# Moving the weight blocks' casts and low parts behind the instruction that follows the former block's last product

## The chip, the cores and the metric

The kernel runs on one core of one Trainium2 chip. The metric is the device time of one execution in microseconds. TensorE (PE) multiplies, VectorE (DVE) and ScalarE (ACT) do elementwise work, SyncE (SP) issues the loads, and all run side by side, each through its own list of instructions.

## What is computed

A block of two layers on 256 latent and 256 context tokens, model width 1024. In each layer: a SwiGLU FFN at half step, four token mixers side by side (attention, Fourier, a convolution module, a short gated convolution) that are merged by gates, and a second FFN at half step. Each part is normalised and modulated first. In short:

```python
def ffn_half(x, mod, slot, g, w13, w2):
    h = modulated_norm(x, mod, slot, g)
    a, b = jnp.split(h @ w13, 2, axis=-1)
    return x + 0.5 * mod[:, :, 3 * slot + 2] * ((jax.nn.silu(a) * b) @ w2)
...
    gates = jax.nn.sigmoid(g + lw['b_gate']).reshape(B, L, N_BRANCHES, D_MODEL)
    merged = gates[:, :, 0] * y_a + gates[:, :, 1] * y_b + gates[:, :, 2] * y_c + gates[:, :, 3] * y_d
    return merged @ lw['w_o']
```

The context tokens are a prefix of the same trunk; the last layer's mixer and FFN produce the latent tokens alone. All weights are float32.

## The kernel before

Activations lie with channels on the partitions and tokens along the free axis, 512 columns (latent and context) in layer 0 and in the first FFN of layer 1, 256 behind it (258 in the last FFN, which carries two columns more for a late normalisation).

**Weight blocks.** A product in float32 precision is made from three faster ones. A block of weights is 128 x 1024, 512 KB. `wblock` (L177) loads it into `raw` (L179, on SyncE's queue), ScalarE casts it to the rounded type as `whi` (L181), and VectorE subtracts that from `raw` and so makes the low part `wlo` (L183). `mm3` (L187 to L189) then multiplies `whi` with the activation's high part, `whi` with its low part, and `wlo` with its high part. There are four buffers for `raw` and six each for `whi` and `wlo`: the cast of a block can be written once the last product has been done that reads the block six before it. There are 408 blocks.

**FFN.** `ffn` (L565) goes through the 22 tiles of the hidden width in three parts. In each part `project` (L493) takes pairs of blocks, one for the a half and one for the b half of a tile: TensorE multiplies both, then ScalarE takes the Silu of a (L583) and VectorE multiplies it with b (L593), and the product is split into high and low part (L193 on ScalarE, L194 on VectorE). Then `down` (L517) multiplies the part with eight w2 blocks and VectorE adds to the residual stream (L372). `down` has no instruction on ScalarE other than casts, and squares in the last part. In the last FFN the evacuation begins with a multiplication by the late normalisation's factor and a copy of a statistic, both on VectorE (L468, L470), and only then has the Silu its input.

**Mixer.** The mixer of a layer multiplies the input projections, then merges four branches (`merge`, L999): for each output tile a gate projection, whose Tanh is taken on ScalarE (L1011), a product of the branch with a `w_br` block, and the gating on VectorE (L1032, L1036). Attention is pumped in between as a job in steps: a query's scaling and rotary embedding, its split into two halves with DMAs (L868 to L870), scores on TensorE (L896), the row maximum and its negation on VectorE (L900, L903), Exp on ScalarE (L908), reciprocal and scaling on VectorE (L911, L912), transposes on TensorE (L923), copies on ScalarE (L927), values on TensorE (L940).

**Filler.** The modulations of later parts are computed along the way (`ada_later`): VectorE multiplies and sums weight tiles (L318), TensorE adds up rows with a matmul on ones (L297), ScalarE copies the sums (L327), and TensorE transposes them (L331).

**What sets the order.** The code is recorded in program order, and a scheduler then decides from dependencies and its own estimate of times in which order each engine gets its instructions; in the first stretch, up to the first FFN's first pairs, the order on TensorE and SyncE is written by hand. On the chip each engine keeps the order it was given. In the order before, a block's cast stands about where its load is expected to have landed, before or behind other work of ScalarE, as the scheduler finds it best.

Of the kernel before, what the change touches and what calls it, by code (L numbers as in the profile page):

```python
# [14 lines left out]
ALU = mybir.AluOpType  # L15
# [5 lines left out]
KD = D // P  # L21
# [59 lines left out]
def hybrid_block(ctx: ExitStack, tc: tile.TileContext, a, out, dbg=None):  # L81
    nc = tc.nc
# [8 lines left out]
    def nm(s):  # L91
        uid[0] += 1
        return f"{s}_{uid[0]}"
# [79 lines left out]
    def load_tables():  # L173
        nc.sync.dma_start(out=rope_c, in_=a["rope_c"])
        nc.sync.dma_start(out=rope_s, in_=a["rope_s"])

    def wblock(src, n=1024):  # L177
        raw = wp.tile([P, 1024], F32, tag="raw", name=nm("raw"), bufs=RINGS["raw"])
        nc.sync.dma_start(out=raw[:, :n], in_=src)  # L179
        hi = wp.tile([P, 1024], F32R, tag="whi", name=nm("whi"), bufs=RINGS["whi"])  # L180
        nc.scalar.copy(hi[:, :n], raw[:, :n])  # L181
        lo = wp.tile([P, 1024], F32R, tag="wlo", name=nm("wlo"), bufs=RINGS["wlo"])
        nc.vector.tensor_tensor(out=lo[:, :n], in0=raw[:, :n], in1=hi[:, :n], op=ALU.subtract)  # L183
        return hi, lo

    def mm3(ps, wh, wl, xh, xl, first, last):
        nc.tensor.matmul(ps, lhsT=wh, rhs=xh, start=first, stop=False)  # L187
# [170 lines left out]
    def cols(s):  # L358
        return slice(s * S, (s + 1) * S)
# [133 lines left out]
    def project(units, u, T, evac, group=1, halves=False, mid=None):  # L493

        for g in range(0, len(units), group):
            some = [(name, src if isinstance(src, list) else [src]) for name, src in units[g : g + group]]
            for i in range(max(len(src) for _, src in some)):
                ws = [wblock(src[i]) for _, src in some]  # L500
                if i == 0:
                    pss = [pmm() for _ in some]
                for n, c in enumerate([cols(s) for s in range(2)] if halves else [slice(0, T)]):
                    o = slice(c.start + i * T, c.stop + i * T)
                    turns = [(k, w) for k in range(KD) for w in zip(ws, pss)]
                    if n == 1:
                        turns = [(k, w) for w in zip(ws, pss) for k in range(KD)]
                    for k, ((hi, lo), ps) in turns:
                        if mid and k == KD // 2:
                            mid()  # L510
                            mid = None
                        kc = slice(k * P, (k + 1) * P)
                        mm3(ps[:, o], hi[:, kc], lo[:, kc], u[k][0][:, c], u[k][1][:, c], k == 0, k == KD - 1)
            for (name, _), ps in zip(some, pss):
                evac(name, ps)

    def down(blocks, parts, NB, G, last, nxt, group=1, filler=None):  # L517
# [12 lines left out]
        for g, count in starts:  # L530
            ws = [blocks(m) for m in range(g, g + count)]
            pss = [pmm() for _ in ws]
            if count == 1:
                mms(ws[0], pss[0], whole)
            else:
                for k in range(n):
                    kc = slice(k * P, (k + 1) * P)
                    for w, ps in zip(ws, pss):
                        mm3(
                            ps[:, whole], w[0][:, kc], w[1][:, kc], parts[k][0][:, whole], parts[k][1][:, whole],  # L540
                            k == 0, k == n - 1,
                        )
            for i, ps in enumerate(pss):
                for s in range(NB):
                    residual(g + i, s, ps, G, last)
                if last and NB == 1:
                    nxt.tile(g + i)
            if not last and filler:
                filler(count)
        if not last:  # L550
            return
        if split_last:
            ws = [blocks(m) for m in range(m1, KD)]
            pss = [pmm() for _ in ws]
            for s in range(2):
                for i, (w, ps) in enumerate(zip(ws, pss)):
                    mms(w, ps, cols(s))
                    residual(m1 + i, s, ps, G, True)
                nxt.stat(s)
            nxt.apply(0)  # L560
        else:
            nxt.stat(0)
            nxt.apply(0)
# [59 lines left out]
    def mixer(l, NB, norm, nxt, filler):  # L623
# [375 lines left out]
        def merge(b, parts, rate, t=0):  # L999
# [4 lines left out]
            for m0 in range(0, KD, per_unit):  # L1004
# [16 lines left out]
                for i, m in enumerate(ms):  # L1021
                    if m % per == 0:
                        blocks = wblock(a["w_br"][l, 2 * b + (m // per) if b < 3 else 6 + m // per])
                    hi, lo = blocks
                    o = ps[:, i * T : (i + 1) * T]
                    for k in range(nk):
                        c = ((m % per) * nk + k) * P
                        xh, xl = parts[k]
                        mm3(o, hi[:, c : c + P], lo[:, c : c + P], xh[:, :T], xl[:, :T], k == 0, k == nk - 1)

                tot = total[m0 // per_unit]
                nc.vector.scalar_tensor_tensor(  # L1032
# [30 lines left out]
    first = []  # L1063
# [4 lines left out]
    def begin_first(ns, ks):  # L1068
        for k in ks:
            kc = slice(k * P, (k + 1) * P)  # L1070
            for n in ns:
                (hi, lo), ps = first[n]
                mm3(ps, hi[:, kc], lo[:, kc], *mix.u[k], k == 0, k == KD - 1)

    def first_norm(k):
        ada.pick(k)
# [201 lines left out]
```

## Time and profile before

| | us |
|---|---|
| median of three runs | 2042.12 |
| range of these | 2039.0 to 2043.8 |
| the profiled execution's own time | 2041.15 |
| its span, first to last instruction | 2039.0 |
| TensorE busy | 2002.6 (98%) |
| VectorE busy | 1337.0 (66%) |
| ScalarE busy | 735.3 (36%) |

The profile comes from one execution. Busy time is time in which an instruction ran; matmuls overlap, and their ends are modelled, so that the distance from start to start tells more of the pace than the duration does. "Idle before" is the time for which an engine did nothing ahead of an instruction, with the instruction that released it. The mean granted clock of TensorE was 0.995 of full speed.

### The profile page before, as it was taken

To read this page: it belongs to the slowest core of one execution; us is meant where nothing else is said; L and a number is where in the kernel's file an instruction comes from. 1 tells how busy PE (TensorE), PEld (TensorE's weight loads), DVE (VectorE), ACT (ScalarE), POOL (GpSimd) and SP (SyncE) were. 2 spreads that over 40 slices of the span, in tenths; PEclk is the share of its full clock that TensorE was granted. 3 is DMA by queue.
4 is the path that set the end of the run, shared out by engine and by line. 5 is a ranking of instruction groups with operands and counts; after the bars stand their busy time and mean duration, and the time that the engine had idled before them with its cause. 6 is when DMAs were issued, how large, how long until landed. Compare 5 with 4: busy or idle time off the path is not lost.

```text
span 2039.0 us, 28106 instructions
## 1 busy us (share of the span) xinstructions
PE 2002.6 (98%) x11034; PEld 1709.0 (84%) x11034; DVE 1337.0 (66%) x2390; ACT 735.3 (36%) x1142; POOL 5.1 (0%) x30
## 2 busy tenths in 40 slices
PE   7999999999999999999999999999999999999998
PEld 4888878888887778888888888888888999899997
DVE  5886697676766554788578455553424878767665
ACT  3322322333344443432222234222223445655443
POOL 0000000000000000000000000000000000000000
PEclk9999999999999999999999999999999999999999
DMA  7755466433222222266457442642323454446562
GB/s 281 245 175 188 150 208 187 146 96 99 83 83 88 77 65 92 73 204 199 151 178 244 151 124 88 198 137 83 115 84 109 138 164 143 134 133 200 180 184 91
DMA packets 83492, 294.08 MB, mean 144 GB/s; under 512 B 9504, under 2 KB 10144, under 8 KB 83360
## 3 DMA queue, kind: packets, MB, share of 16 engines
q1 hardware_dynamic: 83072, 292.07, 45.9%
q8 instruction: 87, 1.43, 0.3%
q14 instruction: 45, 0.37, 0.1%
q10 hardware_dynamic: 288, 0.22, 0.0%
HBM read 289.10 MB, written 1.05 MB: 142 GB/s over the span
## 4 chain that ended last, share of the span: by engine, by line
PE 96%; DVE 2%; ACT 1%; issue 0%; DMA 0%; DVEq 0%; ACTq 0%
PE mm L187 30%; PE mm L188 30%; PE mm L189 30%; PE aux L940 1%; PE aux L896 1%; PE aux L923 1%; PE aux L297 1%; PE aux L783 1%; PE aux L219 0%; DVE wlo L183 0%; PE aux L254 0%; PE aux L808 0%; ACT whi L181 0%; ACT s L908 0%; PE aux L769 0%
## 5 line engine op out<-in xcount | busy, mean ns | idle before, releaser
L187 PE MATMUL mm<-s,whi 128*128 128x512 f32 (+2 forms) x3354 | 1168.9, 349 | 3.0 <-ACT s L423 1.4
L188 PE MATMUL mm<-s,whi 128*128 128x512 f32 (+2 forms) x3354 | 1165.1, 348 | 0.2
L189 PE MATMUL mm<-s,wlo 128*128 128x512 f32 (+2 forms) x3354 | 1163.7, 347 | 0.0
L181 ACT CAST whi<-raw 128x1024 fp32r<-128x1024 f32 (+1 forms) x408 | 419.3, 1031 | 1041.5 <-PE mm L188 811.0
L183 DVE TENSOR_TENSOR wlo<-raw,whi 128x1024 fp32r<-128x1024 f32 (+1 forms) x408 | 488.0, 1202 | 368.1 <-ACT whi L181 363.1
L187 PEld LDWEIGHTS mm<-s,whi 128*128 128x128 f32 x3354 | 634.7, 190 | 97.5 <-issue 8.4
L188 PEld LDWEIGHTS mm<-s,whi 128*128 128x128 f32 x3354 | 636.4, 190 | 79.1 <-issue 1.5
L189 PEld LDWEIGHTS mm<-s,wlo 128*128 128x128 f32 x3354 | 636.1, 190 | 78.6 <-issue 0.8
L318 DVE SCALAR_TENSOR_TENSOR s<-ada,cw,s 128x512 f32<-128x512 f32 x392 | 269.1, 748 | 44.2 <-DMA ada<-in_w_ada 43.9
L372 DVE SCALAR_TENSOR_TENSOR xt<-mm,modG,xt 128x256 f32<-128x256 f32 x192 | 84.6, 480 | 116.6 <-PE mm L189 116.3
L193 ACT CAST s<-s 128x512 fp32r<-128x512 f32 (+1 forms) x104 | 59.4, 571 | 75.9 <-DVE s L593 52.4
L711 DVE SCALAR_TENSOR_TENSOR s<-pad,dw_h,s 128x512 f32<-128x512 f32 (+1 forms) x120 | 74.0, 617 | 2.4 <-DVE sm L210 0.4
L194 DVE TENSOR_TENSOR s<-s,s 128x512 fp32r<-128x512 f32 (+1 forms) x104 | 65.1, 626 | 3.8 <-ACT s L193 3.8
L423 ACT ACTIVATE s<-s,mod 128x256 fp32r<-128x256 f32 x80 | 39.4, 507 | 40.5 <-DVE s L419 40.4
L593 DVE TENSOR_TENSOR s<-s,mm 128x512 f32<-128x512 f32 x66 | 45.0, 682 | 3.5 <-PE mm L189 2.7
L900 DVE TENSOR_REDUCE sm<-aux 128x1 f32<-128x512 f32 (+1 forms) x48 | 28.6, 596 | 24.1 <-PE aux L896 24.0
L908 ACT ACTIVATE s<-aux,sm,sm 128x512 f32<-128x512 f32 (+1 forms) x48 | 33.9, 707 | 26.2 <-DVE sm L903 26.1
L468 DVE TENSOR_TENSOR s<-mm,s 128x256 f32<-128x256 f32 x44 | 18.1, 420 | 36.5 <-PE mm L189 36.5
L583 ACT ACTIVATE s<-mm 128x512 f32<-128x512 f32 x66 | 38.8, 589 | 5.9 <-PE mm L189 5.9
L1032 DVE SCALAR_TENSOR_TENSOR s<-s,mm 128x512 f32<-128x512 f32 x48 | 32.8, 684 | 9.6 <-PE mm L189 8.5
L424 DVE SCALAR_TENSOR_TENSOR s<-s,mod,s 128x256 fp32r<-128x256 f32 x80 | 37.8, 484 | 1.7 <-ACT s L423 1.7
L367 ACT ACTIVATE s<-xt 128x256 f32<-128x256 f32 x70 | 26.7, 409 | 27.7 <-DVE xt L372 27.7
(128 smaller groups left out, 715.1 us busy)
## 6 DMA issues: line engine op xcount, KB each, us to landing
raw<-in_w SPq DMA_DIRECT2D x208, 512.0 KB, 4.3
ada<-in_w_ada SPq DMA_DIRECT2D x144, 512.0 KB, 4.1
raw<-in_w_in SPq DMA_DIRECT2D x100, 512.0 KB, 3.7
raw<-in_w SPq DMA_DIRECT2D x64, 448.0 KB, 4.0
raw<-in_w_br SPq DMA_DIRECT2D x20, 512.0 KB, 3.6
raw<-in_w_o SPq DMA_DIRECT2D x16, 512.0 KB, 3.6
xt<-in_xt SPq DMA_DIRECT2D x4, 512.0 KB, 6.0
s<-s SPq DMA_DIRECT2D x16, 128.0 KB, 2.2
```

What stands on the lines that cost most here:

```text
L181: nc.scalar.copy(hi[:, :n], raw[:, :n])
L183: nc.vector.tensor_tensor(out=lo[:, :n], in0=raw[:, :n], in1=hi[:, :n], op=ALU.subtract)
L187: nc.tensor.matmul(ps, lhsT=wh, rhs=xh, start=first, stop=False)
L188: nc.tensor.matmul(ps, lhsT=wh, rhs=xl, start=False, stop=False)
L189: nc.tensor.matmul(ps, lhsT=wl, rhs=xh, start=False, stop=last)
L193: nc.scalar.copy(hi[:, :n], src)
L194: nc.vector.tensor_tensor(out=lo[:, :n], in0=src, in1=hi[:, :n], op=ALU.subtract)
L318: nc.vector.scalar_tensor_tensor(out=t, in0=src, scalar=cs, in1=t, op0=ALU.mult, op1=ALU.add)
L372: nc.vector.scalar_tensor_tensor(out=xt[:, m, c], in0=ps[:, c], scalar=G[:, m, s : s + 1], in1=xt[:, m, c], op0=ALU.mult, op1=ALU.add,)
L423: nc.scalar.activation(hi[:, c], z, AF.Identity, bias=B[:, k, s : s + 1])
L593: nc.vector.tensor_tensor(out=h[:, :T], in0=s[:, :T], in1=ps[:, :T], op=ALU.mult)
L711: nc.vector.scalar_tensor_tensor(out=ov, in0=h[:, :NB, j : j + S], scalar=dw_h[:, l, i, j : j + 1], in1=ov, op0=ALU.mult, op1=ALU.add,)
```

## The change

`wblock` gives each block a number, and `spent` notes, at the place in the program where a block's last product stands, how many instructions have been recorded by then. When block i is made, `wblock` looks through what was recorded since block i - 6 was spent, and takes on ScalarE the first instruction that is no cast of a block, and on VectorE the first that is no low part. The cast and the low part of block i get a dependency on that instruction, without a semaphore: it only sets the order in which the scheduler may put them on their engine. If nothing was recorded on that engine in between, or block i - 6 isn't spent yet, there is no such dependency.

```diff
+    spent_at = []
+    parts_of_blocks = set()
+
+    def spent(*ws):
+        for w in ws:
+            spent_at[w[2]] = len(nc.cur_bb.bb.instructions)
+
     def wblock(src, n=1024):
...
         hi = wp.tile([P, 1024], F32R, tag="whi", name=nm("whi"), bufs=RINGS["whi"])
-        nc.scalar.copy(hi[:, :n], raw[:, :n])
         lo = wp.tile([P, 1024], F32R, tag="wlo", name=nm("wlo"), bufs=RINGS["wlo"])
-        nc.vector.tensor_tensor(out=lo[:, :n], in0=raw[:, :n], in1=hi[:, :n], op=ALU.subtract)
-        return hi, lo
+        i = len(spent_at)
+        spent_at.append(None)
+        before = None
+        if i >= RINGS["whi"] and spent_at[i - RINGS["whi"]] is not None:
+            before = nc.cur_bb.bb.instructions[spent_at[i - RINGS["whi"]] :]
+        for ins in (
+            nc.scalar.copy(hi[:, :n], raw[:, :n]),
+            nc.vector.tensor_tensor(out=lo[:, :n], in0=raw[:, :n], in1=hi[:, :n], op=ALU.subtract),
+        ):
+            ins = ins.ins
+            parts_of_blocks.add(ins.name)
+            for x in before or ():
+                if x.engine == ins.engine and x.name not in parts_of_blocks:
+                    tc.add_manual_dep(
+                        ins, x.name,
+                        mybir.DependencyInfo(mybir.DependencyClass.NoSync, mybir.DependencyReason.DATA),
+                        reason="buffer",
+                    )
+                    break
+        return hi, lo, i
...
                         mm3(ps[:, o], hi[:, kc], lo[:, kc], u[k][0][:, c], u[k][1][:, c], k == 0, k == KD - 1)
+                spent(*ws)
             for (name, _), ps in zip(some, pss):
                 evac(name, ps)
...
                             k == 0, k == n - 1,
                         )
+            spent(*ws)
             for i, ps in enumerate(pss):
                 for s in range(NB):
                     residual(g + i, s, ps, G, last)
```

`merge` calls `spent` after the last tile that a `w_br` block serves, the last part of `down` after the second half of the tokens, the written first stretch at a block's last product.

The lines of the kernel shift with the change: the cast is L198 in the new numbering, the low part L199, the products L214 to L216, the Silu L614, the split L220 and L221, the scores L927, the query halves L899, the Exp L939, the transposes L954, the copies L958, the gate's Tanh L1042.

**ScalarE in an FFN, at about 302 us of the trace before.** The names are those of the tiles: `whi_421` and `whi_424` belong to the second pair behind a `down`, `whi_435` and `whi_438` to the third, `mm_412` is the a half of the first pair. Before:

```order
L181 CAST whi_407_2280<-raw_406_2278 128x1024
L181 CAST whi_410_2286<-raw_409_2284 128x1024
L181 CAST whi_421_2362<-raw_420_2360 128x1024
L181 CAST whi_424_2368<-raw_423_2366 128x1024
L181 CAST whi_435_2444<-raw_434_2442 128x1024
L181 CAST whi_438_2450<-raw_437_2448 128x1024
L583 ACTIVATE s_414_2340<-mm_412_2290 128x512
L181 CAST whi_449_2526<-raw_448_2524 128x1024
L193 CAST s_416_2344<-s_415_2342 128x512
L181 CAST whi_452_2532<-raw_451_2530 128x1024
```

and now:

```order
L198 CAST whi_407_2280<-raw_406_2278 128x1024
L198 CAST whi_410_2286<-raw_409_2284 128x1024
L614 ACTIVATE s_414_2340<-mm_412_2290 128x512
L198 CAST whi_421_2362<-raw_420_2360 128x1024
L198 CAST whi_424_2368<-raw_423_2366 128x1024
L220 CAST s_416_2344<-s_415_2342 128x512
L198 CAST whi_435_2444<-raw_434_2442 128x1024
L198 CAST whi_438_2450<-raw_437_2448 128x1024
L198 CAST whi_449_2526<-raw_448_2524 128x1024
L198 CAST whi_452_2532<-raw_451_2530 128x1024
```

The Silu of the first pair has moved ahead of the casts of the second, third and fourth.

**ScalarE in the mixer of layer 0, at about 650 us.** `aux_943` and `aux_948` hold scores, `mm_957` a gate. Before:

```order
L181 CAST whi_1006_5397<-raw_1005_5395 128x1024
L1011 ACTIVATE s_933_5091<-mm_937_5098,b_gate_h_98 128x512
L868 CAST s_940_5131<-s_646_3698 64x512
L181 CAST whi_1025_5472<-raw_1024_5470 128x1024
L181 CAST whi_1041_5553<-raw_1040_5551 128x1024
L868 CAST s_941_5135<-s_646_3698 64x512
L908 ACTIVATE s_946_5155,sm_947_5156<-aux_943_5148,sm_945_5153,sm_803_4542 128x512
L181 CAST whi_1061_5634<-raw_1060_5632 128x1024
L908 ACTIVATE s_951_5167,sm_952_5168<-aux_948_5160,sm_950_5165,sm_803_4542 128x512
L1011 ACTIVATE s_953_5172<-mm_957_5179,b_gate_h_98 128x512
```

and now:

```order
L1042 ACTIVATE s_933_5091<-mm_937_5098,b_gate_h_98 128x512
L892 ACTIVATE s_646_3698<-s_646_3698,par_70 128x512
L899 CAST s_940_5131<-s_646_3698 64x512
L899 CAST s_941_5135<-s_646_3698 64x512
L939 ACTIVATE s_946_5155,sm_947_5156<-aux_943_5148,sm_945_5153,sm_803_4542 128x512
L939 ACTIVATE s_951_5167,sm_952_5168<-aux_948_5160,sm_950_5165,sm_803_4542 128x512
L1042 ACTIVATE s_953_5172<-mm_957_5179,b_gate_h_98 128x512
L958 COPY s_958_5205<-aux_960_5207 128x2x128
```

The four casts 1006, 1025, 1041 and 1061 have left the stretch; they come behind the Exps of later scores.

**ScalarE and TensorE in the mixer of layer 1, at about 1700 us.** `aux_2469` and `aux_2474` hold scores, `aux_2493` takes the transposes of the first of them, `mm_2487` and `mm_2499` are a branch product and a gate projection. ScalarE before:

```order
L181 CAST whi_2497_13917<-raw_2496_13915 128x1024
L181 CAST whi_2501_13948<-raw_2500_13946 128x1024
L1011 ACTIVATE s_2455_13679<-mm_2459_13686,b_gate_h_98 128x256 x2
L181 CAST whi_2523_14053<-raw_2522_14051 128x1024
L181 CAST whi_2527_14084<-raw_2526_14082 128x1024
L868 CAST s_2465_13750<-s_2305_12775 64x512
L868 CAST s_2466_13754<-s_2305_12775 64x512
L181 CAST whi_2549_14179<-raw_2548_14177 128x1024
L181 CAST whi_2564_14225<-raw_2563_14223 128x1024
L908 ACT_TABLE_LOAD
L908 ACTIVATE s_2472_13782,sm_2473_13783<-aux_2469_13775,sm_2471_13780,sm_2454_13675 128x512
L908 ACTIVATE s_2477_13794,sm_2478_13795<-aux_2474_13787,sm_2476_13792,sm_2454_13675 128x512
L1011 ACTIVATE s_2479_13801<-mm_2483_13808,b_gate_h_98 128x256 x2
```

and now:

```order
L1042 ACTIVATE s_2455_13679<-mm_2459_13686,b_gate_h_98 128x256 x2
L899 CAST s_2465_13750<-s_2305_12775 64x512
L899 CAST s_2466_13754<-s_2305_12775 64x512
L939 ACT_TABLE_LOAD
L939 ACTIVATE s_2472_13782,sm_2473_13783<-aux_2469_13775,sm_2471_13780,sm_2454_13675 128x512
L939 ACTIVATE s_2477_13794,sm_2478_13795<-aux_2474_13787,sm_2476_13792,sm_2454_13675 128x512
L1042 ACTIVATE s_2479_13801<-mm_2483_13808,b_gate_h_98 128x256 x2
L198 CAST whi_2497_13917<-raw_2496_13915 128x1024
L958 COPY s_2491_13892<-aux_2493_13894 128x2x128
L958 COPY s_2492_13893<-aux_2493_13894 128x2x128
L198 CAST whi_2501_13948<-raw_2500_13946 128x1024
```

The casts 2497 and 2501 have gone from ahead of the query halves to behind both Exps and the gate. TensorE about these scores before, where 18 products of `mm_2499` have been made already and more follow:

```order
L896 MATMUL aux_2469_13775<-s_2393_13341,s_2465_13750 128x512
L896 MATMUL aux_2469_13775<-s_2392_13340,s_2465_13750 128x512
L896 MATMUL aux_2474_13787<-s_2393_13341,s_2465_13750 128x512
L896 MATMUL aux_2474_13787<-s_2392_13340,s_2465_13750 128x512
L187 MATMUL mm_2499_13921<-s_2260_12511,whi_2497_13917 128x256
L188 MATMUL mm_2499_13921<-s_2261_12512,whi_2497_13917 128x256
L189 MATMUL mm_2499_13921<-s_2260_12511,wlo_2498_13919 128x256
L187 MATMUL mm_2499_13921<-s_2262_12513,whi_2497_13917 128x256
L188 MATMUL mm_2499_13921<-s_2263_12514,whi_2497_13917 128x256
```

and now:

```order
L927 MATMUL aux_2474_13787<-s_2392_13340,s_2465_13750 128x512
L215 MATMUL mm_2487_13871<-s_2432_13553,whi_2489_13874 128x256
L216 MATMUL mm_2487_13871<-s_2431_13552,wlo_2490_13875 128x256
L214 MATMUL mm_2487_13871<-s_2443_13628,whi_2489_13874 128x256
L215 MATMUL mm_2487_13871<-s_2444_13629,whi_2489_13874 128x256
L216 MATMUL mm_2487_13871<-s_2443_13628,wlo_2490_13875 128x256
L954 MATMUL aux_2493_13894<-ident_74,s_2472_13782 128x128 x4
L954 MATMUL aux_2494_13901<-ident_74,s_2477_13794 128x128 x4
L214 MATMUL mm_2499_13921<-s_2248_12499,whi_2497_13917 128x256
L215 MATMUL mm_2499_13921<-s_2249_12500,whi_2497_13917 128x256
L927 MATMUL aux_2503_13978<-s_2395_13347,s_2466_13754 128x512
L927 MATMUL aux_2503_13978<-s_2394_13346,s_2466_13754 128x512
```

The products of `mm_2499` come behind the transposes, and five products stand between scores and transposes.

## Rows read from the trace of the kernel before

**Rows 1.** The page, busy time by engine (share of the span, instructions), and the chain that ended last by engine.

```profile
PE 2002.6 (98%) x11034; PEld 1709.0 (84%) x11034; DVE 1337.0 (66%) x2390; ACT 735.3 (36%) x1142; POOL 5.1 (0%) x30
...
PE 96%; DVE 2%; ACT 1%; issue 0%; DMA 0%; DVEq 0%; ACTq 0%
```

**Rows 2.** The page, costliest groups of instructions: line, engine, operation, out<-in, count | busy us, mean ns of one | idle time just before them and what ended most of it. The casts and the low parts.

```profile
L181 ACT CAST whi<-raw 128x1024 fp32r<-128x1024 f32 (+1 forms) x408 | 419.3, 1031 | 1041.5 <-PE mm L188 811.0
L183 DVE TENSOR_TENSOR wlo<-raw,whi 128x1024 fp32r<-128x1024 f32 (+1 forms) x408 | 488.0, 1202 | 368.1 <-ACT whi L181 363.1
```

**Rows 3.** Timeline of ScalarE (ACT) in the mixer of layer 0: start us, us, engine, line, operation, out<-in, count, and in brackets the idle time before it with its releaser.

```profile
650.41 1.05 ACT L181 CAST whi<-raw 128x1024 fp32r<-128x1024 f32 x1 [5.75 <-PE mm L188]
651.49 0.62 ACT L868 CAST s<-s 64x512 fp32r<-64x512 f32 x1
652.13 0.78 ACT L908 ACTIVATE s<-aux,sm,sm 128x512 f32<-128x512 f32 x1
...
654.78 0.78 ACT L908 ACTIVATE s<-aux,sm,sm 128x512 f32<-128x512 f32 x1 [0.85 <-DVE sm L903]
...
655.55 0.68 ACT L1011 ACTIVATE s<-mm,b_gate_h 128x512 f32<-128x512 f32 x1
```

**Rows 4.** Timeline of TensorE (PE) in the same stretch.

```profile
651.57 0.39 PE L189 MATMUL mm<-s,wlo 128*128 128x512 f32 x1
654.67 1.11 PE L923 MATMUL aux<-ident,s 128*128 128x128 f32 x4 [2.71 <-DVE s L912]
656.27 0.80 PE L187 MATMUL mm<-s,whi 128*128 128x512 f32 x1 [0.49 <-ACT s L1011]
```

**Rows 5.** Windows around it: stretch in us, its length, busy time of each engine, PEclk (the granted clock), share of DMA, GB/s.

```profile
651.00:656.00 5.00, 2.07 (x9) 1.17 (x7) 4.41 (x9) 4.10 (x8) 0.00 (x0) 0.80 0.43 111
656.00:660.00 4.00, 3.73 (x14) 2.79 (x14) 2.87 (x7) 1.88 (x7) 0.00 (x0) 0.50 0.47 157
```

**Rows 6.** Timeline of TensorE at 302 us: 302.48 is the last product of the first pair, 302.71 the first of the second pair.

```profile
302.48 0.39 PE L189 MATMUL mm<-s,wlo 128*128 128x512 f32 x1
302.71 0.39 PE L187 MATMUL mm<-s,whi 128*128 128x512 f32 x1
```

**Rows 7.** Timeline of ScalarE before and at the same place: the casts of the second pair's two blocks, and the first pair's Silu.

```profile
287.74 1.05 ACT L181 CAST whi<-raw 128x1024 fp32r<-128x1024 f32 x1 [16.39 <-DMA raw<-in_w]
291.22 1.05 ACT L181 CAST whi<-raw 128x1024 fp32r<-128x1024 f32 x1 [2.43 <-DMA raw<-in_w]
...
302.23 0.60 ACT L583 ACTIVATE s<-mm 128x512 f32<-128x512 f32 x1 [4.67 <-PE mm L189]
```

**Rows 8.** Timeline of VectorE (DVE) at the same place: the multiply with the Silu, and two steps of the adaLN sums.

```profile
302.98 0.69 DVE L593 TENSOR_TENSOR s<-s,mm 128x512 f32<-128x512 f32 x1
303.58 1.41 DVE L318 SCALAR_TENSOR_TENSOR s<-ada,cw,s 128x512 f32<-128x512 f32 x2
```

**Rows 9.** Timeline of TensorE at 1353 us: four matmuls on ones (eight records), and the product behind them.

```profile
1352.71 1.06 PE L297 MATMUL aux<-s,ones_w 128*32 128x512 f32 x8
1353.71 0.50 PE L187 MATMUL mm<-s,whi 128*128 128x512 f32 x1
```

**Rows 10.** Timeline of ScalarE at the same place: the copy of the sums that those matmuls made.

```profile
1353.89 0.59 ACT L327 COPY s<-aux 128x512 f32<-128x512 f32 x1 [0.26 <-PE aux L297]
```

**Rows 11.** Timeline of VectorE and of TensorE at 1911 us, in the last FFN, and then the group of the Silu of that FFN.

```profile
1911.57 0.42 DVE L468 TENSOR_TENSOR s<-mm,s 128x256 f32<-128x256 f32 x1 [3.26 <-PE mm L189]
...
1911.72 0.28 PE L187 MATMUL mm<-s,whi 128*128 128x258 f32 x1
...
L583 ACT ACTIVATE s<-s,sm 128x256 f32<-128x256 f32 x22 | 11.1, 506 | 1.7 <-DVE sm L470 1.7
```

**Rows 12.** Timeline of TensorE in the mixer of layer 1, about the scores (L896) and the transposes (L923) of its first queries; 42 products stand from 1699.76 to 1704.68, 0.12 us from start to start.

```profile
1698.76 1.16 PE L896 MATMUL aux<-s,s 128*128 128x512 f32 x4 [0.67 <-DMA s<-s]
1699.76 0.28 PE L187 MATMUL mm<-s,whi 128*128 128x256 f32 x1
...
1704.68 0.28 PE L189 MATMUL mm<-s,wlo 128*128 128x256 f32 x1
1705.23 0.44 PE L923 MATMUL aux<-ident,s 128*128 128x128 f32 x2 [0.27 <-DVE s L912]
```

**Rows 13.** Timeline of VectorE and then of ScalarE in the same stretch: the first reduction, a tap of the convolution, the negation, the scaling of both; then the first Exp.

```profile
1699.50 0.69 DVE L900 TENSOR_REDUCE sm<-aux 128x1 f32<-128x512 f32 x1 [0.55 <-PE aux L896]
1700.11 0.47 DVE L711 SCALAR_TENSOR_TENSOR s<-pad,dw_h,s 128x256 f32<-128x256 f32 x1
1700.50 0.21 DVE L903 TENSOR_SCALAR sm<-sm,sm 128x1 f32<-128x1 f32 x1
...
1704.70 0.87 DVE L912 TENSOR_SCALAR s<-s,sm 128x512 f32<-128x512 f32 x2
...
1702.96 0.78 ACT L908 ACTIVATE s<-aux,sm,sm 128x512 f32<-128x512 f32 x1
```

**Rows 14.** Timeline of TensorE at 852 us, the window about it, and a window after 1592 us.

```profile
852.21 0.61 PE L219 MATMUL aux<-ones_d,acc 128*128 128x1 f32 x4 [1.79 <-DVE acc L368]
...
850.00:853.00 3.00, 1.21 (x11) 1.00 (x10) 1.84 (x6) 2.19 (x4) 0.00 (x0) 1.00 0.46 175
...
1592.00:1596.00 4.00, 3.94 (x20) 3.73 (x20) 3.90 (x18) 1.93 (x5) 0.00 (x0) 0.59 0.08 31
```

**Rows 15.** Timeline of TensorE at 1735 us, in the mixer of layer 1.

```profile
1735.81 0.38 PE L187 MATMUL mm<-s,whi 128*128 128x256 f32 x1 [0.47 <-ACT s L1011]
```

More of the change, by code (lines that the diff above doesn't have):

```diff
@@ L507, in project @@
                         turns = [(k, w) for w in zip(ws, pss) for k in range(KD)]
-                    for k, ((hi, lo), ps) in turns:
+                    for k, ((hi, lo, _), ps) in turns:
                         if mid and k == KD // 2:
@@ L557, in down @@
                     mms(w, ps, cols(s))
+                    if s == 1:
+                        spent(w)
                     residual(m1 + i, s, ps, G, True)
@@ L1023, in merge @@
                         blocks = wblock(a["w_br"][l, 2 * b + (m // per) if b < 3 else 6 + m // per])
-                    hi, lo = blocks
+                    hi, lo, _ = blocks
                     o = ps[:, i * T : (i + 1) * T]
@@ L1029, in merge @@
                         mm3(o, hi[:, c : c + P], lo[:, c : c + P], xh[:, :T], xl[:, :T], k == 0, k == nk - 1)
+                    if m % per == per - 1:
+                        spent(blocks)
                 tot = total[m0 // per_unit]
@@ L1071, in begin_first @@
             for n in ns:
-                (hi, lo), ps = first[n]
+                (hi, lo, _), ps = first[n]
                 mm3(ps, hi[:, kc], lo[:, kc], *mix.u[k], k == 0, k == KD - 1)
+                if k == KD - 1:
+                    spent(first[n][0])
     def first_norm(k):
```

## The prediction

> **What bounds the kernel now.** I began with the page: busy times, then the chain that ended last. TensorE is busy for 2002.6 of 2039.0 us, and 96% of the chain runs over it [rows 1]. The kernel is matmul bound, only 36.4 us of the span are TensorE's idle time, and an edit that leaves all 11034 matmuls in place can win no more than those. It can lose without limit, because each cast or low part that comes late stops TensorE.
>
> The costliest groups show what the edit is about: ScalarE's casts of weight blocks (L181) stand idle for 811.0 us in front of "PE mm L188", which is the wait for the last product that reads the buffer's former block; VectorE's low parts (L183) stand idle for 363.1 us behind those casts [rows 2]. Each engine works through its own stream in order, so what is queued behind such a cast waits too, although ready.
>
> The one place where I find that this holds up TensorE is the mixer of layer 0 at 650 us. ScalarE's timeline has a cast there with 5.75 us of idle time before it, and then, at once, a query cast, an Exp, a second Exp and a gate [rows 3]. TensorE ends a product started at 651.57 and starts again at 654.67, on a transpose that wants the scaled Exp; it stops again until 656.27 for the gate [rows 4]. In the windows the granted clock stands at 0.80 and then at 0.50 [rows 5], the lower of the two levels, 1.2 GHz. The cluster holds 2.7 + 0.5 us of idle time and, of the 3.73 us busy at half clock, about 1.9 that full clock would not have taken, with the edges of the gaps some 5.7 in all.
>
> Everywhere else the early casts are harmless, even useful. At 302 us, where `down` gives way to the next pair of `project`, TensorE goes from one pair to the next in the usual pace of 0.227 us per product [rows 6]: the two casts that the new pair needs were made at 287.74 and 291.22, eleven to fifteen us earlier [rows 7].
>
> **The change, part by part.** Nothing is added or taken away: same matmuls, casts, low parts, waits and buffers. What changes is where casts and low parts stand. Over most of the program they move by one instruction or two and are still some 100 products ahead of use, 22 us at 0.227; I cost these at nothing. If that cover went, each would cost what the places below cost.
>
> Casts lose their cover where a block's buffer was last used in `down`. ScalarE has no other instruction during `down`, so the next one that follows a w2 block's last product is the Silu of the first new pair. The casts of the second pair, made 11 us early before, now stand behind that Silu, and the Silu wants the last product of the first pair. TensorE has 3 products left by then. Such a transition comes twice in each of four FFNs, eight in all.
>
> At 302: the Silu runs from 302.23 for 0.60, so the first cast (1.05) ends at about 303.83; the first product stood at 302.71 [rows 6, 7], so +1.12. The second cast ends 0.95 later, 0.5 after TensorE has done the two products that the new order puts in between. Low part: VectorE multiplies from 302.98 (0.69), does one adaLN step (1.41 for two) [rows 8], then the low part (1.2), to about 305.5: +0.25. Together +1.9. The transition at 1484.9 has no adaLN step: +1.6. At 183.0 and 999.6 four matmuls on ones stand in the gap; a row of 1353 shows them at 1.0 us between 1352.71 and the next product at 1353.71 [rows 9], so that only the second cast shows, +0.6 and +0.5. At 1118 the first cast stays early: +0.05. At 1353.7 three casts go behind the copy at 1353.89 (0.59) [rows 10]; the transposes of that copy are moved ahead of the products, so TensorE waits about 0.65 for the copy, and 0.5 and 0.55 for two casts: +1.7.
>
> In the last FFN the evacuation begins on VectorE: L468 at 1911.57 for 0.42, then the statistic's copy, then Silu (506 ns), then the cast, to 1913.6; the product stood at 1911.72 [rows 11]: +1.9. Its low part comes behind the multiply and the cast, to 1914.8: +1.0. Two of these: +5.8. The eight sum to 0.6 + 1.9 + 0.5 + 0.05 + 1.7 + 1.6 + 5.8 = +12.2.
>
> The mixer of layer 1 loses cover in another way. Before, 42 products from 1699.76 to 1704.68 lie between the scores and the transposes, while reduction, Exp and scaling go on [rows 12, 13]. Of these 30 read two blocks whose casts now stand behind both Exps and the gate, and they go behind the transposes with the rest; five other products (0.6 us) remain. From the scores' first result the path is reduction 0.69, negation 0.2 behind a tap of 0.48, Exp 0.78 and its accumulator, reciprocal and scaling 0.48 [rows 13]: with the gaps between them 3.4 to 4.3, less 0.6 of cover 2.8 to 3.7, say 3.3. The cast and low part behind it add about 1.0. Off come 0.67 + 0.27 of before's idle time and its edges, 1.3 [rows 12]: +3.0, or 2 to 4.6, as the scores' query DMA may come sooner or later. A gap of this size has two likenesses: 2.71 at 654.67 [rows 4], followed by half clock, and 1.79 at 852.21, after which the window reads 1.00 [rows 14]. I side with the larger: half clock for as long as after 1592 (window at 0.59, some 3.4 us), of which half is lost: +1.7. At 1735.81, where a gate already stops TensorE for 0.47 [rows 15], three casts and a low part come behind a query's scaling: one low part of 1.2 and a rest of 0.3 for the casts, +1.5 (0 to 3).
>
> The gain: in the 650 cluster casts go behind the Exps. The Exp still waits for reductions, and the gate and the transposes for a freed bank, so about 2.9 us of 5.7 stay; I take -2.0 (-1 to -5.7, the whole cluster).
>
> Sum: 12.2 + 3.0 + 1.7 + 1.5 - 2.0 = +16.4. The profiled execution took 2041.15 (span 2039.0 plus 2.15 around it), 1 below the median of 2042.12: 2057.6, so **2058**.
>
> [...]
>
> **Rivals.** *Only the stall goes.* For it: the idle time of 811.0 us is real, and a delayed cast whose lead stays positive costs nothing. Then the transitions and layer 1 are free and 2.0 to 5.7 comes off: 2035.5 to 2039, faster. It decides if the first product of the second pair still starts within 0.3 us of the previous one. Against it: Silu, cast and product are a chain with 3 products of cover. 0.05.
>
> *Gain and loss cancel*, or the moved casts find their gaps already covered by late evacuations, and only two or three transitions show: 2038 to 2046, no change. 0.09.
>
> *The clock falls too.* The gaps of 1.9 with 1.0 behind it in the last FFN, and those near 1.1 with 0.5 behind, pull the clock down as 2.71 did. Half of 3.4 us at five to eight places is +8 to +14: 2066 to 2072. For it the window at 0.50 [rows 5]; against it 1.79 at 1.00 [rows 14]. 0.16.
>
> *Transitions alone.* Layer 1's scores are reached while their query DMA is still on its way, the taps run meanwhile, and nothing is lost there: 2041.15 + 12.2 - 2.0 = 2051, with 2046 to 2053 around it. 0.15.
>
> *The forecast*, 2053 to 2065: 0.55.
>
> **How the numbers follow.** What a measurement can tell from no change is 0.2%, 4 us: slower begins at 2046.2, faster below 2038. Slower holds the forecast, the clock and the transitions alone, 0.86; faster nearly all of the first rival, 0.05; no change 0.09. The range leaves out the first rival, most of the second and the top of the third: 2045 to 2071.
>
> **What would show it.** At each of the eight transitions a TensorE wait on "ACT whi" or "DVE wlo" of 0.5 to 1.9 us, together 10 to 15 where before has almost none; the wait of the transposes on L912 near 1700 grown from 0.27 to some 3 us, with a window below 1.00 after it; the wait of 2.71 at 654.67 cut; ScalarE's 811.0 mostly turned into waits on evacuations. I am wrong if TensorE's idle time stays near 36 us, or if it grows elsewhere: in `merge` of layer 0, say.

## The result

The changed kernel takes 2063.15 us (median; 2062.4 to 2064.86) against 2042.46 before in the same comparison: a ratio of 1.0107, with a 95% interval from 1.0095 to 1.0119. It is slower by 20.7 us, where 2058 us, or about 16 more, had been forecast, and it lies within the range.

The page of the changed kernel, its busy times, its chain and the groups that answer to [rows 1] and [rows 2] (columns as there):

```profile
PE 2009.2 (97%) x11034; PEld 1714.4 (83%) x11034; DVE 1341.7 (65%) x2390; ACT 722.6 (35%) x1142; POOL 5.1 (0%) x30
...
PE 92%; DVE 5%; ACT 2%; issue 1%; DMA 1%; DVEq 0%; ACTq 0%; SPq 0%
...
L199 DVE TENSOR_TENSOR wlo<-raw,whi 128x1024 fp32r<-128x1024 f32 (+1 forms) x408 | 481.9, 1199 | 66.9 <-ACT whi L198 62.3
L198 ACT CAST whi<-raw 128x1024 fp32r<-128x1024 f32 (+1 forms) x408 | 408.3, 1030 | 138.8 <-DMA raw<-in_w 44.7
...
L614 ACT ACTIVATE s<-mm 128x512 f32<-128x512 f32 x66 | 39.5, 598 | 540.6 <-PE mm L216 540.6
```

The change does what it says, and that is not worth anything by itself. Of the 811.0 us for which ScalarE's casts stood in front of a full buffer 40.9 are left in the view of its waits; most of the rest stands now in front of the Silu, as a wait for the product (540.6). VectorE's 363.1 us behind the casts are down to 62.3. Yet the span grew from 2039.0 to 2061.4 us, and the share of TensorE in the chain fell from 96 to 92%, with VectorE and ScalarE in its place: TensorE now waits for them. Its idle time grew from 36.4 to 52.2 us, and its busy time by 6.6 for the same matmuls.

For whom it waits is in its own view of waits (engine and line, what it waited for: us in total, times, the longest):

```profile
PE mm L214 <- ACT whi L198: 6.6, 10, 1.7
PE aux L954 <- DVE s L943: 5.4, 3, 3.7
PE mm L216 <- DVE wlo L199: 4.1, 4, 1.9
...
PE aux L927 <- DMA s<-s: 1.6, 1, 1.6
```

Waits of a product for a cast or a low part did not occur in that view of the kernel before; here they are 10.7 us in fourteen places. The longest wait of the transposes grew from 2.71 us, in the mixer of layer 0 [rows 4], to 3.7, and it is in another place now: the mixer of layer 1, where it was 0.27 [rows 12].

To see where the rest is, I took from both traces the start of the last product of every product tile, by the tile's name, and its difference between the two. Where it jumps, time was lost or won. The growth, by stretch of the trace before:

| stretch of the trace before | forecast, us | measured, us |
|---|---|---|
| the first 150 us | 0 | -1.55 |
| transition at 183 | +0.6 | +0.5 |
| transition at 302 | +1.9 | +2.7 |
| end of the first FFN | 0 | -0.5 |
| mixer of layer 0 | -2.0 | -2.1 |
| ends of the second and third FFN, from 850 and 1010 | 0 | +1.7, +2.5 |
| transitions at 999.6 and 1118 | +0.5, +0.05 | +0.5, 0 |
| transitions at 1353.7 and 1484.9 | +1.7, +1.6 | +1.8, +1.7 |
| mixer of layer 1 | +6.2 | +6.3 |
| the two transitions of the last FFN | +2.9, +2.9 | +4.4, +4.25 |

With small steps between these and the roundings (+0.4 in all) they make 22.6 us, the growth of the span (22.4) but for the last instructions. The eight transitions are 15.85 of them. Each column of starts comes from one execution, and not every step belongs to the change: more of that at the end of the part on why the prediction was right, and in the last section.

### The profile page after: what moved, and what is told of

Same layout as the page of the kernel before. It is cut to its first block, busy times and chain, and to the rows that moved or that the text cites. A ratio compares the mean times of both kernels' runs of the same rounds, so it can differ in the third digit from the quotient of the medians.

```text
span 2061.4 us, 28053 instructions
## 1 busy us (share of the span) xinstructions
PE 2009.2 (97%) x11034; PEld 1714.4 (83%) x11034; DVE 1341.7 (65%) x2390; ACT 722.6 (35%) x1142; POOL 5.1 (0%) x30
## 4 chain that ended last, share of the span: by engine, by line
PE 92%; DVE 5%; ACT 2%; issue 1%; DMA 1%; DVEq 0%; ACTq 0%; SPq 0%
PE mm L214 29%; PE mm L216 29%; PE mm L215 29%; PE aux L971 1%; DVE wlo L199 1%; PE aux L954 1%; ACT whi L198 1%; PE aux L927 1%; DVE s L742 1%; PE aux L324 1%; PE aux L246 0%; PE aux L814 0%; DVE s L345 0%; PE aux L281 0%; ACT s L939 0%
## 5 line engine op out<-in xcount | busy, mean ns | idle before, releaser
L214 PE MATMUL mm<-s,whi 128*128 128x512 f32 (+2 forms) x3354 | 1173.5, 351 | 9.2 <-ACT whi L198 6.6
L216 PE MATMUL mm<-s,wlo 128*128 128x512 f32 (+2 forms) x3354 | 1167.2, 348 | 4.1 <-DVE wlo L199 4.1
L214 PEld LDWEIGHTS mm<-s,whi 128*128 128x128 f32 x3354 | 638.6, 191 | 106.3 <-ACT whi L198 17.3
L216 PEld LDWEIGHTS mm<-s,wlo 128*128 128x128 f32 x3354 | 639.5, 191 | 84.2 <-DVE wlo L199 6.1
L199 DVE TENSOR_TENSOR wlo<-raw,whi 128x1024 fp32r<-128x1024 f32 (+1 forms) x408 | 481.9, 1199 | 66.9 <-ACT whi L198 62.3
L198 ACT CAST whi<-raw 128x1024 fp32r<-128x1024 f32 (+1 forms) x408 | 408.3, 1030 | 138.8 <-DMA raw<-in_w 44.7
L614 ACT ACTIVATE s<-mm 128x512 f32<-128x512 f32 x66 | 39.5, 598 | 540.6 <-PE mm L216 540.6
L624 DVE TENSOR_TENSOR s<-s,mm 128x512 f32<-128x512 f32 x66 | 45.1, 684 | 227.3 <-PE mm L216 227.3
L399 DVE SCALAR_TENSOR_TENSOR xt<-mm,modG,xt 128x256 f32<-128x256 f32 x192 | 84.4, 477 | 124.2 <-PE mm L216 123.7
L220 ACT CAST s<-s 128x512 fp32r<-128x512 f32 (+1 forms) x104 | 59.3, 570 | 75.7 <-DVE s L1069 33.2
L221 DVE TENSOR_TENSOR s<-s,s 128x512 fp32r<-128x512 f32 (+1 forms) x104 | 64.8, 623 | 7.1 <-ACT s L220 7.1
L1042 ACT ACTIVATE s<-mm,b_gate_h 128x512 f32<-128x512 f32 (+1 forms) x64 | 35.4, 580 | 89.1 <-PE mm L216 88.3
L939 ACT ACTIVATE s<-aux,sm,sm 128x512 f32<-128x512 f32 (+1 forms) x48 | 33.9, 707 | 35.0 <-DVE sm L934 35.0
L614 ACT ACTIVATE s<-s,sm 128x256 f32<-128x256 f32 x22 | 11.2, 510 | 76.5 <-DVE sm L497 76.5
```

The lines of the kernel that those rows point to most:

```text
L198: nc.scalar.copy(hi[:, :n], raw[:, :n]),
L216: nc.tensor.matmul(ps, lhsT=wl, rhs=xh, start=False, stop=last)
L220: nc.scalar.copy(hi[:, :n], src)
L221: nc.vector.tensor_tensor(out=lo[:, :n], in0=src, in1=hi[:, :n], op=ALU.subtract)
L399: nc.vector.scalar_tensor_tensor(out=xt[:, m, c], in0=ps[:, c], scalar=G[:, m, s : s + 1], in1=xt[:, m, c], op0=ALU.mult, op1=ALU.add,)
L614: nc.scalar.activation(s[:, :T], ps[:, :T], AF.Silu, bias=bias)
```

## The experiments

Each kernel was timed beside the kernel before, whose median was 2040.82, 2040.28 or 2039.9 us in these comparisons and 2042.46 in the first. The ratios allow for that; differences between medians of two comparisons carry up to 2.6 us of it.

**Which blocks: those behind a `down`.** One kernel leaves the rule as it is but takes the notes out of `down`, the other keeps only those.

```diff
-            spent(*ws)
             for i, ps in enumerate(pss):
...
-                    if s == 1:
-                        spent(w)
```

> The rule as it is, but no block that was used in down is noted as spent, so that the blocks behind a down are free again. Theory (the eight FFN transitions carry most of the loss): about 16 of the 20.7 us go away, 2047 us; no wait of TensorE on a cast or a low part at the transitions, while the wait of some 3.7 us for the scaled Exp near 1704 and the shorter stall at 655 stay as in the changed kernel. Rival (the mixers carry the loss): 2058 us or more.

> The counterpart: only blocks that were used in down are noted as spent. Theory: 2058 us, with waits on casts and low parts at the eight transitions as in the changed kernel, the stall of 2.7 us at 655 as in the kernel before, and no new wait near 1704. Rival (the mixers carry the loss): 2042 to 2047 us.

Measured: without `down` 2044.16 us, 1.002 of the kernel before (1.0011 to 1.003); with `down` alone 2057.92, 1.0089 (1.0074 to 1.0104). So some 17 of the 20.7 us hang on the blocks behind a `down` (2047 and 2058 us were said), and the mixers cannot be the main cause. What was left without `down` is in that kernel's waits from 1600 to 1800 us, the mixer of layer 1:

```profile
PE aux L951 <- DVE s L940: 4.0, 2, 3.7
PE mm L216 <- DVE wlo L199: 1.9, 1, 1.9
```

They are the same two waits as in the changed kernel, and no product waits for a cast anywhere in it.

**Which engine: ScalarE.** One kernel has the dependency on ScalarE's casts alone, one on VectorE's low parts alone (with `!=` in place of the second `==`).

```diff
-                if x.engine == ins.engine and x.name not in parts_of_blocks:
+                if x.engine == ins.engine == mybir.EngineType.Activation and x.name not in parts_of_blocks:
```

> The dependency on ScalarE alone, the low parts free. Theory: a low part can't start before its cast, so the late casts carry the loss by themselves: 2057 to 2063 us. Rival (the loss comes from low parts queued behind VectorE's work): under 2048 us.

> The dependency on VectorE alone, the casts free. Theory: the first low part of a transition still stands behind the multiply, so that about half of each transition's wait remains (1.3 us at 302, 2 in the last FFN), but the wait near 1704 goes: 2048 to 2054 us. Rival (the loss comes from low parts): 2060 us or more.

Casts alone: 2063.17 us, 1.0106 (1.0091 to 1.0122), the whole loss. Low parts alone: 2037.52 us, 0.9986 (0.9977 to 0.9996), which is no loss at all; the 0.14% less is under the 0.2% that the prediction took as the least that can be told. My expectation for it missed, and its error teaches something: I had taken the multiply with the Silu (L624) for the instruction that the low part must follow, since I was thinking of ScalarE. But `down` is not empty on VectorE: its residual steps (L399) stand between. VectorE's timeline of that kernel has the second pair's low parts behind a residual and a row of adaLN steps, ahead of the multiply:

```profile
291.40 0.88 DVE L399 SCALAR_TENSOR_TENSOR xt<-mm,modG,xt 128x256 f32<-128x256 f32 x2 [0.94 <-PE mm L216]
292.19 4.72 DVE L345 SCALAR_TENSOR_TENSOR s<-ada,cw,s 128x512 f32<-128x512 f32 x7
296.82 2.36 DVE L199 TENSOR_TENSOR wlo<-raw,whi 128x1024 fp32r<-128x1024 f32 x2
```

They start 4.8 us ahead of the Silu, which stands at 301.60 in that trace; in the kernel before it was 4.3 (297.91 and 302.23). So in the changed kernel the low parts of the transitions are late because their casts are, not by their own rule. One product of that kernel still waits 1.94 us for a low part, at 280.78 inside a `down`; I have not pursued it.

**Which blocks of the mixer of layer 1: two of 408.** The changed kernel, with blocks 2497 and 2501 exempt:

```diff
-        if i >= RINGS["whi"] and spent_at[i - RINGS["whi"]] is not None:
+        if uid[0] not in (2498, 2502) and i >= RINGS["whi"] and spent_at[i - RINGS["whi"]] is not None:
```

> The changed kernel with two blocks of 408 exempt, 2497 and 2501, whose products lay between scores and transposes in the kernel before. Theory: their late casts alone make the wait of 3.7 us near 1704 and the half clock behind it: about 6 us less, 2057 us, and the wait is below 1 us. Rival (the scores come too late for other reasons): 2062 us or more, with the wait still over 2.5 us.

Measured: 2058.33 us, 1.0092 (1.0076 to 1.0108). By the medians that is 4.8 us under the changed kernel, by the ratios about 3, where the expectation said 6; the two intervals overlap, so the total alone does not show it. The trace does: from start to start the mixer of layer 1 costs 2.2 us there in place of 6.3. The wait at the transposes is gone, down to 0.2 us in that kernel's waits from 1600 to 1800 us, but another has grown there from 1.9 to 2.3:

```profile
PE mm L216 <- DVE wlo L199: 2.3, 1, 2.3
...
PE aux L954 <- DVE s L943: 0.2, 1, 0.2
```

So the mechanism holds: the two early casts were worth the long wait. The low part that waits longer, 45 us on, gave a little of it back.

**The last FFN's second pairs: four blocks.** In the same way 3002, 3005, 3146 and 3149 were exempt.

> The changed kernel with four blocks exempt, the second pairs behind the two downs of the last FFN (3002, 3005, 3146, 3149). Theory: their waits (2.8 us each) and the half clock behind them (1.4 us each) go: about 8.5 us less, 2054 to 2055 us, and no wait of TensorE on a cast or low part after 1800 us. Rival (the third pairs become late in their place): 2060 us or more.

Measured: 2054.41 us, 1.007 (1.0056 to 1.0084), 8.7 us under the changed kernel by the medians and about 7.5 by the ratios, near the 8.5 expected, and the intervals do not overlap; after 1800 us no product waits for a cast or a low part there. The third pairs did not become late in their place.

**Versions that might be better.** The rule without `down` and without layer 1's mixer:

```diff
+        if stage[0] != 1 and i >= RINGS["whi"] and spent_at[i - RINGS["whi"]] is not None:
...
-            spent(*ws)
...
     def mixer(l, NB, norm, nxt, filler):
+        stage[0] = l
```

> As the run without down, and the rule also off for blocks made in the mixer of layer 1. Theory (losses at the scores and behind them in layer 1, gain in the mixer of layer 0): the 6 us lost there go, the gain of 4 us up to the end of layer 0 stays: 2036 to 2039 us, under the kernel before. Rival (what layer 1's mixer lost would be lost elsewhere once the order moves): 2043 us or more.

2038.82 us, 0.999 (0.998 to 1.0): the loss of the mixer is gone and did not come back elsewhere, as the theory said, but the gain is at the edge of what can be told from none. The rule with a look ahead, which takes as the instruction to follow only one that was recorded before the block two earlier was made:

```diff
-            before = nc.cur_bb.bb.instructions[spent_at[i - RINGS["whi"]] :]
+            before = nc.cur_bb.bb.instructions[spent_at[i - RINGS["whi"]] : made_at[i - 2]]
```

> The rule with a look ahead: the instruction that a cast or low part must follow is taken only if it was recorded before the block two before it was made. Theory: the second pair's casts are free of the Silu of the first pair, so that the transitions cost nothing, while layer 1's scores still do: 2044 to 2048 us. Rival (third and later pairs become late instead): 2055 us or more.

2045.81 us, 1.0031 (1.002 to 1.0042): that takes the transitions' loss away without naming `down` at all (by start to start none of the eight costs over 0.1 us in its trace), and leaves layer 1's. Low parts by the rule except in layer 1's mixer, with casts by the rule in layer 0's:

```diff
...
+                if ins.engine == mybir.EngineType.Activation and stage[0] != 0:
+                    break
...
```

> Low parts by the rule everywhere but in the mixer of layer 1, casts by the rule in the mixer of layer 0 alone. Theory: the gain of the low parts (0.1%) and that of the casts in layer 0's mixer add up, since each is a stall of its own: 2033 to 2037 us. Rival (both remove the same stall at 655): 2037 us or more.

2038.38 us, 0.9995 (0.9985 to 1.0005): no difference that can be told; the gains of the two did not add. And the rule for three of layer 0's merges only (`stage[0]` is set in `merge` for b > 0, nothing is noted in `down`):

> The rule for blocks made in the second to fourth merge of layer 0's mixer alone, down not noted. Theory (the stall at 655 is cut by those casts, and the wait of 1.65 us for the query DMA near 565 came from earlier blocks): the gain at 655 stays and the wait near 565 is under 1 us: 2034 to 2038 us. Rival (the wait near 565 comes with the gain): 2038 to 2041 us.

2041.21 us, 0.9996 (0.9987 to 1.0005): no difference. From start to start the query DMA near 565 costs 1.10 us in that trace, where the version without `down` and layer 1's mixer had 1.65. That is no sign that earlier blocks had a part in it: the version without `down` alone has the same order as that one on TensorE, VectorE and ScalarE up to 1597 us, and it has 1.10 too (idle times of 0.94 and 1.49 for the DMA). The total came out above both of my ranges, and the run does not settle where the wait comes from. The best of all, low parts alone, is 0.14% under the kernel before with an interval that just leaves 1 out; as the best of ten kernels, and under 0.2%, I don't count it as a gain.

## Why the prediction was right

**The place and the mechanism.** The prediction's main step, that the second pair behind each `down` loses the lead of its casts to the first pair's Silu, stands as written. TensorE's timeline of the changed kernel at 302, only the rows with idle time, and then ScalarE's:

```profile
302.88 0.50 PE L214 MATMUL mm<-s,whi 128*128 128x512 f32 x1 [0.94 <-ACT whi L198]
303.82 0.50 PE L214 MATMUL mm<-s,whi 128*128 128x512 f32 x1 [0.21 <-ACT whi L198]
305.22 0.50 PE L216 MATMUL mm<-s,wlo 128*128 128x512 f32 x1 [0.66 <-DVE wlo L199]
```

```profile
301.29 0.60 ACT L614 ACTIVATE s<-mm 128x512 f32<-128x512 f32 x1 [30.96 <-PE mm L216]
301.79 1.98 ACT L198 CAST whi<-raw 128x1024 fp32r<-128x1024 f32 x2
```

ScalarE did nothing for 30.96 us before that Silu, while the buffers of both blocks had long been free: in the trace before those casts stand eleven to fifteen us ahead of it [rows 7]. The first product came 1.10 us late by the distance from start to start (1.12 said), the second block 0.38 (0.5 said). The low part cost 0.83 instead of 0.25: VectorE's multiply began at 302.69 behind four adaLN steps that the order had put there, and so did not start with the Silu's end. This is the part of that place that was mis-sized; besides, the first product behind each of the three gaps takes about 0.1 more than the pace (302.88 to 303.21, where it is 0.23), which the sum left out. The other transitions outside the last FFN came within 0.1 us of the sum.

**The last FFN.** The waits were as said, 1.87 and 0.92 by start to start for 1.9 and 1.0. The two cost 4.4 and 4.25 instead of 2.9 each because TensorE's clock fell behind them. The prediction had this as its third rival, for the gaps of 1.9 with 1.0 behind, and put it outside the likeliest case: the mechanism was right, and the term mis-sized by 1.4 us a place. Windows of the changed kernel, and then of the kernel with `down` alone, each about the first of them (PEclk before the last two columns):

```profile
1925.00:1929.00 4.00, 1.54 (x10) 1.12 (x10) 2.85 (x8) 2.96 (x5) 0.00 (x0) 0.95 0.00 0
1929.00:1933.00 4.00, 4.00 (x23) 4.00 (x24) 3.48 (x4) 2.20 (x3) 0.00 (x0) 0.62 0.76 192
```

```profile
1921.00:1925.00 4.00, 1.55 (x11) 1.13 (x10) 2.95 (x8) 3.06 (x5) 0.00 (x0) 1.00 0.00 0
1925.00:1929.00 4.00, 4.00 (x35) 4.00 (x34) 3.39 (x3) 2.24 (x3) 0.00 (x0) 1.00 0.66 203
```

In the 4 us behind the gap TensorE did 23 matmuls in one and 35 in the other, with the clock at 0.62 and at 1.00. The rival's other half was wrong: at 302 and 1484 no window shows a lower clock.

**The mixer of layer 1** came to +6.3 for 6.2 said, but from parts of other sizes. ScalarE's timeline shows the path of [rows 13] without its cover, the Exps, the gate and then the cast, and TensorE's the wait:

```profile
1705.04 0.78 ACT L939 ACTIVATE s<-aux,sm,sm 128x512 f32<-128x512 f32 x1 [3.93 <-DVE sm L934]
1705.71 0.19 ACT L939 ACTIVATION_READ_ACCUMULATOR s<-aux,sm,sm 128x1 f32 x1
1706.55 0.78 ACT L939 ACTIVATE s<-aux,sm,sm 128x512 f32<-128x512 f32 x1 [0.65 <-DVE sm L934]
1707.22 0.19 ACT L939 ACTIVATION_READ_ACCUMULATOR s<-aux,sm,sm 128x1 f32 x1
1707.32 0.83 ACT L1042 ACTIVATE s<-mm,b_gate_h 128x256 f32<-128x256 f32 x2
1708.03 1.05 ACT L198 CAST whi<-raw 128x1024 fp32r<-128x1024 f32 x1
```

```profile
1704.40 0.28 PE L216 MATMUL mm<-s,wlo 128*128 128x256 f32 x1
1708.41 1.97 PE L954 MATMUL aux<-ident,s 128*128 128x128 f32 x8 [3.73 <-DVE s L943]
```

The wait is 3.73 where 3.3 was taken. The 1.0 for a cast and a low part behind it did not show: no product there waits for either. The clock stands at 0.50 in the window from 1708 to 1712, as assumed from the larger likeness [rows 4], but it was low for longer, with 0.84 and 0.81 in the windows before and behind it. The term at 1735 was a wait of a low part of 1.9, at 1752 of the new trace, instead of 1.5 for all, and the clock fell behind that too, which the sum did not have:

```profile
1708.00:1712.00 4.00, 3.59 (x14) 3.07 (x15) 3.93 (x7) 3.52 (x8) 0.00 (x0) 0.50 0.00 0
1712.00:1716.00 4.00, 4.00 (x30) 4.00 (x29) 3.52 (x5) 2.60 (x3) 0.00 (x0) 0.81 0.83 263
1756.00:1760.00 4.00, 4.00 (x29) 4.00 (x28) 3.94 (x6) 1.27 (x2) 0.00 (x0) 0.76 0.86 240
```

That such parts came within 0.1 us of the sum owes much to luck. The run with two blocks free shows that the casts caused the first wait and the low clock behind it: its windows from 1704 to 1716 are all at 1.00.

**The gain** at 655 was taken as 2.0 and came as 2.1 for the whole mixer, but from two steps that were not told apart: between 567 and 755 of the trace before 3.9 us came back, since the cluster's gaps shrank to 1.49 and 0.40 and the windows of 4 us from 652 to 664 all have a clock of 1.00, where [rows 5] had 0.80 and 0.50; and a new wait of 1.64 for the query DMA near 569 took 1.9 away. So the place gave about twice what was taken, and that the whole agrees is luck. Nor is all of the 3.9 the order's: the kernel with two blocks free has the same order up to 1692 us and the same two gaps, and yet its window from 660 to 664 is at 0.68, and it wins 2.4 there. TensorE's timeline of the changed kernel, the rows with idle time:

```profile
656.60 0.66 PE L954 MATMUL aux<-ident,s 128*128 128x128 f32 x4 [1.49 <-DVE s L943]
657.66 0.50 PE L214 MATMUL mm<-s,whi 128*128 128x512 f32 x1 [0.40 <-ACT s L1042]
```

```profile
569.35 1.17 PE L927 MATMUL aux<-s,s 128*128 128x512 f32 x4 [1.64 <-DMA s<-s]
```

**What the sum left out** is what I had costed at nothing. The end of an FFN, where a norm follows, lost 1.7 us from 850 and 2.5 from 1010 on. At 850 nothing came later: TensorE waits 1.55 for the statistic's sum and then 0.28, where it waited 1.79 at once [rows 14], and only the clock behind it fell, which the last section takes up. At 1223 a low part stands now in front of the last residual step, where it stood 1.6 us ahead of it before; the statistic's matmul, in TensorE's timeline first of the kernel before and then of the changed one, waits longer for it:

```profile
1223.90 0.61 PE L219 MATMUL aux<-ones_d,acc 128*128 128x1 f32 x4 [1.12 <-DVE acc L368]
```

```profile
1226.17 0.60 PE L246 MATMUL aux<-ones_d,acc 128*128 128x1 f32 x4 [1.74 <-DVE acc L395]
```

The clock is at 0.86 and 0.72 in the two windows of 4 us behind it, where it stayed at 1.00 before. The kernel with the look ahead waits 1.76 at this place and keeps 1.00 from 1222 to 1230, and there it loses 0.8; so some 0.8 of the 2.5 is the late low part, and the rest goes with the clock. The first 150 us won 1.55, also unforeseen. Of that 0.95 came before 51 us, where the order on TensorE, VectorE and ScalarE is still that of before; the kernel with `down` alone, which has it up to 155 us, is 2.98 ahead of the kernel before at the same point. So this part is the execution's and not the change's. The errors are of both signs, and that the total came within five us owes something to that.

## What to carry to other kernels

An engine that stands in front of a full buffer for two fifths of the time is not a fault as long as nothing that is wanted stands behind it. Work made ahead of its use is the lead that covers evacuations; before a wait at a queue's head is removed, look up for each place what comes next on that engine, what that waits for, and how many instructions of the bound engine are left by then. A rule that orders by a buffer's last use should also hold a minimum lead, and it should be asked separately of each engine: the same rule was harmless on VectorE, where a residual step stands between, and cost 1% on ScalarE, where nothing does. And a clock that was read behind one gap in one trace is one draw: look at it in several executions before a sum rests on it.

## What the runs showed of the hardware that I had not expected

The same two waits, to a hundredth of a us, were followed by half clock in one kernel and by none in another. TensorE's timeline of the changed kernel, and of the kernel with `down` alone, rows with idle time:

```profile
1927.54 0.39 PE L214 MATMUL mm<-s,whi 128*128 128x258 f32 x1 [1.70 <-ACT whi L198]
1928.80 0.58 PE L216 MATMUL mm<-s,wlo 128*128 128x258 f32 x1 [0.75 <-DVE wlo L199]
```

```profile
1923.44 0.39 PE L214 MATMUL mm<-s,whi 128*128 128x258 f32 x1 [1.70 <-ACT whi L198]
1924.70 0.39 PE L216 MATMUL mm<-s,wlo 128*128 128x258 f32 x1 [0.75 <-DVE wlo L199]
```

The waits are alike at 1.70 and 0.75, and so is the work ahead of them (36 matmuls in the 4 us before the window of each); the product behind takes 0.58 in the one and 0.39 in the other, and the place costs 4.4 us in the one and 3.0 in the other. Nor does the order of the instructions settle it. At the end of the second FFN the changed kernel and the kernel with the last FFN's four blocks free have the same order on TensorE, VectorE and ScalarE, up to 1914 us, and the same wait. TensorE's row of each, with a window behind it:

```profile
851.39 0.61 PE L246 MATMUL aux<-ones_d,acc 128*128 128x1 f32 x4 [1.55 <-DVE acc L395]
...
853.00:857.00 4.00, 3.91 (x21) 3.90 (x21) 4.00 (x19) 2.16 (x5) 0.00 (x0) 0.57 0.00 0
```

```profile
852.62 0.61 PE L246 MATMUL aux<-ones_d,acc 128*128 128x1 f32 x4 [1.54 <-DVE acc L395]
...
854.00:858.00 4.00, 3.92 (x33) 3.71 (x32) 4.00 (x19) 2.32 (x5) 0.00 (x0) 1.00 0.02 8
```

The place costs 1.7 us in the first and 0.2 in the second. The wait of 1.79 from which the prediction took its smaller likeness [rows 14] comes out both ways too: in the kernel with the rule for three of layer 0's merges the same wait, at 849.57, has a clock of 0.60 in the window from 852 to 856. So whether a gap of one to two us brings the lower clock is settled neither by the gap nor by the order, and a sum over such gaps has an uncertainty of about 1.5 us a place that no single trace shows. What settles it these runs leave open.
